# MLP of a hybrid decoder layer: order of a split, of copies and of one modulation changed

## The chip, the cores and the metric

The kernel runs on one core of one Trainium2 chip. The metric is the device time of one execution in microseconds. Three runs of the kernel before took 1068.99, 1073.79 and 1074.58 us (median 1073.79); the profiled execution took 1073.34 us.

## The reference

One decoder layer on 1024 tokens of 1024 channels, in float32:

```python
mod = (silu(c) @ ada_w + ada_b)
sh1, sc1, g1, sh2, sc2, g2 = split(mod, 6)
u = rmsnorm(h, norm_mix_w) * (1 + sc1) + sh1
...                                   # four token mixers on u @ w_in: pool, gated conv, SSD, S5
h = h + g1 * (groups @ w_out)
v = rmsnorm(h, norm_mlp_w) * (1 + sc2) + sh2
h = h + g2 * (square(relu(v @ w1)) @ w2)      # w1: 1024 x 4096, w2: 4096 x 1024
out = rmsnorm(h, final_norm_w)
```

The six vectors of the modulation are numbered s = 0 to 5 here: s = 3 is sh2, s = 4 sc2, and s = 5 is g2, the gate of the MLP.

## The kernel before

**Precision.** Every matrix operand is split into a high and a low part (ScalarE casts the high part, VectorE subtracts to get the low one: `split_w`, L114, and `split_half`, L1005 to L1007), and every product is three matmuls (`three`, L1078 to L1080): high by high, high by low, low by high.

**Order.** Nothing sets the order by hand but the program's text. A planner goes through the instructions by priority (their place in the text; those under `tc.high_priority()` come ahead of all others that are ready), simulates the engines, and fixes one order for each engine's queue and for SP's queue of DMA issues. On the chip each queue runs in that order. Buffers are slots of a tag with a fixed count (`BUFS`): "u" 16, "x" 8, "m" 4, "g5" 3 of 1024 columns, "s" and "t" 8 of 512; "w" 8 and "ws" 2 for weights. A tile waits for its slot until all readers of the earlier tile there are done. PSUM has eight banks, four of tag "pj" and four of "ms".

**Modulation.** Each of the six vectors is eight blocks of 128; a block is a load of 512 KB of `adaT` and one VectorE instruction with a running sum against `cond` (`ada_block`, L326). s = 0, 1, 2 and 4 are done early. The list `between` (L550) holds s = 5 and then s = 3; `ada_some(8)` takes the first eight after the S5 mixer, and `prepare` (L929) takes one more behind each of its w_out loads, through the same two "ws" buffers. `project` (L951) adds a group's output projection to h.

**v.** `to_v` normalises h for 128 tokens; after every fourth, `v_half` (L1012 on) transposes, and writes v's quarter operands "11", "21" (first half of the tokens), then "12", "22". The difference x12 - x11 and those after it, and their splits into operands T1 to T4, are made in `combinations` (L1028), called after the first weight pair.

**MLP, first product.** Sixteen pairs of weight blocks: pair 0 plainly, pairs 1 to 15 by a scheme of seven products in place of eight (`hidden`, L1099). A pair has three stages, divided by `yield`: the first multiplies "11" (bank `px`) and "21" (`py`); the second T2 (into `px` again) and T1 (`pz`), and T3 (into `px` again); the third T4 (into `px`) and "22" (into `pz`). Before a product is added into `px`, ScalarE copies what stands there (`u1`, L1125; `u2`, L1138; `u3`, L1147), and the next matmul into `px` waits for that copy. Each product is 12 matmuls of 512 columns. A pair's two raw weight tiles are "g5" tiles where n is even, "ws" tiles where it is odd (loads at L1105). A pair's results (squared ReLU and their sums) are stored to DRAM (L1058) for the second product. The loop at L1168 runs stage 2 of pair n, stage 1 of n + 1, stage 3 of n.

**MLP, second product.** Again seven products, in steps (`Step`, L1190) of 24 matmuls into four banks `q`. A step loads its operands a and b (L1182) into "u" tiles, splits them into four tiles of 1024 columns, "w" by default, and sets aside t12 = b12 - b11 in an "x" tile; loads run four steps ahead, splits two. T1 and T2 of the first product are in "x" tiles too, T3 in "m".

Of the kernel before, what the change touches and what calls it, by code (L numbers as in the profile page):

```python
# [16 lines left out]
ADD, SUB, MUL = ALU.add, ALU.subtract, ALU.mult  # L17
# [3 lines left out]
NB = 8  # L21
# [30 lines left out]
def body(ctx: ExitStack, tc: tile.TileContext, x, c, pk, adaT, w_x, w_zd, w_pl, w_gl, w_in, w_out, w1, w2, fnw, out):  # L52
    nc = tc.nc
    V, A, PE, G, SY = nc.vector, nc.scalar, nc.tensor, nc.gpsimd, nc.sync
# [8 lines left out]
    def gran(name, dt=F32, tag="m"):  # L63
        return gp.tile([P, 1024], dt, tag=tag, name=name, bufs=BUFS[tag])

    def half(name, dt=F32, tag="s"):
        return gp.tile([P, 512], dt, tag=tag, name=name, bufs=BUFS[tag])
# [4 lines left out]
    def small(name, w):  # L72
        return sm.tile([P, w], F32, tag=name, name=name)
# [4 lines left out]
    H = (slice(0, 512), slice(512, 1024))  # L78
# [56 lines left out]
    def tt(a, b, op, o=None, eng=None):  # L135
        if o is None:
            o = tmp(a.shape[1])
        (eng or V).tensor_tensor(out=o, in0=a, in1=b, op=op)  # L138
        return o
# [168 lines left out]
    cond = gran("cond")  # L308
# [6 lines left out]
    mod = small("mod", 48)  # L315
# [231 lines left out]
                PE.matmul(ps[h], w_[:, ks], u_[:, H[h]], start=(a and first), stop=(b and last))  # L547


    between = [(s_, j) for s_ in (5, 3) for j in range(NB)]  # L550

    def ada_some(n):
        for s_, j in between[:n]:
# [48 lines left out]
    for h in range(2):  # L602
        if h == 0:
            ps = [bank(f"pjx{i}{h}", "pj" if i < 4 else "ms") for i in range(NX)]
        for k in range(NB):
            if h == 0:
                t = load_xw(k)
# [27 lines left out]
            for i in range(NX):  # L635
                wh, wl, o = xw_of(k, i)
# [31 lines left out]
    for b in range(2):  # L668
        ps = proj(8 + b, f"s5{b}")
        v8_ = Vt[b].rearrange("p (m c) -> p c m", m=8)  # L670
        for h in range(2):
# [3 lines left out]
                     in_=Vt[b].rearrange("p (m c) -> p m c", m=8))  # L675
# [167 lines left out]
    def norm_of(grp, y, eps, tag):  # L843
        ps = bank(f"bss{grp}", "pj")
        sq = [gran(f"sq{grp}{b}", tag=tag) for b in range(2)]
        for h in range(2):
            for b in range(2):
                A.activation(out=sq[b][:, H[h]], in_=y[b][h], func=AF.Square)
            tt(sq[0][:, H[h]], sq[1][:, H[h]], ADD, o=sq[0][:, H[h]])
        for tb in range(NB):  # L850
            PE.matmul(ps[:, tb:tb + 1], sq[0][:, tb * P:(tb + 1) * P], one, start=True, stop=True)
        r = small(f"br{grp}", 8)
        V.tensor_scalar(out=r, in0=ps[:, 0:8], scalar1=1.0 / 256, scalar2=eps, op0=MUL, op1=ADD)
        G.tensor_tensor(out=r, in0=r, in1=mhalf.to_broadcast([P, 8]), op=ALU.pow)
        return r
# [73 lines left out]
    def prepare(grp, y, last=False):  # L929
        yh, yl = [], []  # L930
        for b in range(2):
            if last:
                hi, lo = ([half(f"y{n_}{grp}{b}{h}", F32R, t_) for h in range(2)] for n_, t_ in ("hs", "lt"))
            else:
                hi, lo = (gran(f"y{n_}{grp}{b}", F32R, "u") for n_ in "hl")
                hi, lo = ([t[:, H[h]] for h in range(2)] for t in (hi, lo))
            for h in range(2):
                A.copy(out=hi[h], in_=y[b][h])
                V.tensor_tensor(out=lo[h], in0=y[b][h], in1=f(hi[h]), op=SUB)
            yh.append(hi)  # L940
            yl.append(lo)
        wo = []
        for b in range(2):
            kb = grp * 2 + b
            t = load_w(w_out[kb], f"wo{kb}")
            V.scalar_tensor_tensor(out=t, in0=t, scalar=pv("bw", kb, kb + 1), in1=g1row, op0=MUL, op1=MUL)
            wo.append(split_w(t, f"wo{kb}"))
            ada_some(1)
        return grp, yh, yl, wo

    def project(prep, r, after_tb=None):  # L951
        grp, yh, yl, wo = prep
        for tb in range(NB):
            ts_ = slice((tb % 4) * P, (tb % 4 + 1) * P)
            for h in range(2):
                ps = bank(f"o{grp}{tb}{h}", "pj")
                for b in range(2):
                    yh_, yl_ = yh[b][tb // 4][:, ts_], yl[b][tb // 4][:, ts_]
                    PE.matmul(ps, yh_, wo[b][0][:, H[h]], start=(b == 0), stop=False)  # L959
                    PE.matmul(ps, yh_, wo[b][1][:, H[h]], start=False, stop=False)  # L960
                    PE.matmul(ps, yl_, wo[b][0][:, H[h]], start=False, stop=(b == 1))  # L961
                hh = ht[tb][:, H[h]]
                if r is None:
                    tt(hh, ps, ADD, o=hh)
                else:
                    V.scalar_tensor_tensor(out=hh, in0=ps, scalar=r[:, tb:tb + 1], in1=hh, op0=MUL, op1=ADD)
            if after_tb is not None:
                after_tb(tb)
# [9 lines left out]
    pb = prepare(1, yb)  # L978
    rb = []
    project(pa, ra, lambda tb: rb.append(norm_of(1, yb, EPS, "m")) if tb == 3 else None)  # L980
    pc = prepare(2, [[t[:, H[h]] for h in range(2)] for t in yc], True)
    project(pb, rb[0])

# [15 lines left out]
    def operand(e, j):  # L999
        if (e, j) not in vop:  # L1000
            vop[e, j] = gran(f"v{e}_{j}", F32R, RTAG[e])
        t = vop[e, j]
        return t[:, H[0]], t[:, H[1]]

    def split_half(hi, lo, t):  # L1005
        A.copy(out=hi, in_=t)  # L1006
        V.tensor_tensor(out=lo, in0=t, in1=f(hi), op=SUB)  # L1007
# [18 lines left out]
            V.tensor_tensor(out=lo, in0=t, in1=f(hi), op=SUB)  # L1026

    def combinations():  # L1028
        for j in range(KQ):
            x11, x12, x21, x22 = (vx[e, j] for e in ("11", "12", "21", "22"))  # L1030
            tt(x12, x11, SUB, o=x11)
            tt(x22, x12, SUB, o=x12)
            tt(x22, x11, SUB, o=x22)
            split_half(*operand("T2", j), x22)
            tt(x21, x22, SUB, o=x21)
        for j in range(KQ):
            split_half(*operand("T1", j), vx["11", j])
        for e, x_ in (("T3", "12"), ("T4", "21")):
            for j in range(KQ):
                split_half(*operand(e, j), vx[x_, j])  # L1040
# [58 lines left out]
    def hidden(n):  # L1099

        tag = "ws" if n % 2 else "g5"
        t0, t1 = (gran(f"w1_{n}{e}", tag=tag) if tag == "g5" else
                  wp.tile([P, 1024], F32, tag=tag, name=f"w1_{n}{e}", bufs=2) for e in range(2))
        for e, t in enumerate((t0, t1)):
            SY.dma_start(out=t, in_=w1[2 * n + e])  # L1105
        l11, l12, l21, l22 = t0[:, H[0]], t0[:, H[1]], t1[:, H[0]], t1[:, H[1]]

        def split(nm, t):
            o = wp.tile([P, 1024], F32R, tag="w", name=f"wo{nm}_{n}", bufs=8)
            o = o[:, H[0]], o[:, H[1]]  # L1110
            with tc.high_priority():
                split_half(*o, t)
            return o

        def product(o, e, ps, first):
            for j in range(KQ):
                three(ps, [cut(t, j * P) for t in o], operand(e, j), first and j == 0, j == KQ - 1, not first)

        sum_ = lambda a, b, op, o: tt(a, b, op, o=o)
        c = {}  # L1120
        x_, y_, z_ = bank(f"px{n}", "pj"), bank(f"py{n}"), None
        o11, o12 = split("11", l11), split("12", l12)
        product(o11, "11", x_, True)
        u1 = half(f"u1_{n}", tag="t")
        A.copy(out=u1, in_=x_)  # L1125
        product(o12, "21", y_, True)
        c["11"] = tt(u1, y_, ADD, o=u1)
        squared(u1)
        with tc.high_priority():
            tt(l21, l22, ADD, o=l21)  # L1130
            tt(l21, l11, SUB, o=l11)
        s2, s1 = split("S2", l11), split("S1", l21)
        with tc.high_priority():
            tt(l12, l11, SUB, o=l12)
        yield
        product(s2, "T2", x_, False)
        u2 = half(f"u2_{n}", tag="s")
        A.copy(out=u2, in_=x_)  # L1138
        z_ = bank(f"pz{n}")
        product(s1, "T1", z_, True)  # L1140
        o22 = split("22", l22)
        with tc.high_priority():
            tt(l22, l11, SUB, o=l22)
        s3 = split("S3", l22)
        product(s3, "T3", x_, False)
        u3 = half(f"u3_{n}", tag="s")
        A.copy(out=u3, in_=x_)  # L1147
        c["22"] = tt(u3, z_, ADD, o=u3)
        squared(u3)
        yield  # L1150
        s4 = split("S4", l12)
        product(o22, "T4", x_, False)
        c["21"] = half(f"c21_{n}", tag="t")
        squared(c["21"], x_)
        product(s4, "22", z_, False)
        c["12"] = tt(u2, z_, ADD, o=u2)
        squared(u2)
        keep_sums(n, c)
        yield
# [8 lines left out]
    for n in range(1, NP - 1):  # L1168
        next(pairs[n])
        next(pairs[n + 1])  # L1170
        next(pairs[n])
    g2r = row_of(5, "g2row")[0]
    next(pairs[NP - 1])

# [85 lines left out]
        return rstd_of(ss, 1.0 / D, EPS, f"rsf{tb}")  # L1260

    s0, s1 = banks("q0_", "pj"), banks("q1_", "ms")
    p1 = [Step("11", "B11", s0, i, True) for i in range(NI)]
    p2 = [Step("12", "B21", s1, i, True) for i in range(NI)]
    s2 = []
    p5 = [Step("S1", "T1", s2, i, True) for i in range(NI)]
# [196 lines left out]
```

## Time and profile before

| | |
|---|---|
| median of three runs | 1073.79 us |
| profiled execution | 1073.34 us |
| its span | 1071.2 us |
| TensorE (PE) busy | 1024.1 us, 4806 matmuls |
| VectorE (DVE) busy | 764.5 us |
| ScalarE (ACT) busy | 499.3 us |
| mean granted TensorE clock | 0.986 of full |

The span is from the first to the last instruction on the core. Busy shares are of the span. PEclk is the granted TensorE clock as a share of full speed. Times of single instructions are counted from the span's start. The mixers take the first 395 us or so, v is made until about 463 us, the MLP's first product runs to about 754 us, the second to the end.

### The profile page before, as it was taken

What the parts mean: (1) busy time and instruction counts of PE and PEld (TensorE: products, weight loads), DVE (VectorE), ACT (ScalarE), POOL (GpSimd) and SP (SyncE); (2) the same over time, 40 slices, a digit from 0 to 9 for tenths busy, and PEclk for the clock granted to TensorE, in tenths of its full rate; (3) what the DMA queues carried; (4) which work ended last, traced back from release to release, by engine and by line L of the source; (5) the groups of instructions that cost most, each with busy time, mean ns of one, the idle gap of its engine ahead of it and who ended that gap; (6) DMA issues with size and microseconds to landing.
All of it is one profiled execution on the core that took longest, in us unless ns stands there. A gap on an engine that the chain in (4) does not pass through costs nothing.

```text
span 1071.2 us, 13218 instructions
## 1 busy us (share of the span) xinstructions
PE 1024.1 (96%) x4806; PEld 836.5 (78%) x4806; DVE 764.5 (71%) x1339; ACT 499.3 (47%) x829; POOL 47.8 (4%) x83
## 2 busy tenths in 40 slices
PE   4989999999999999899999999998999999999997
PEld 3778987776888888688888887886788887777885
DVE  8999958777888878975655656555644766568683
ACT  5634623316634336754645555554443443433542
POOL 2300000000010102000000000000000000000041
PEclk9999999999889999899999999999999999999999
DMA  9873311134611215034444443477975466787112
GB/s 358 320 260 114 118 33 31 63 98 147 250 65 60 79 51 205 21 138 147 151 145 148 157 148 131 153 285 264 387 263 196 156 194 201 253 301 233 55 79 79
DMA packets 61027, 175.08 MB, mean 163 GB/s; under 512 B 6401, under 2 KB 11009, under 8 KB 60962
## 3 DMA queue, kind: packets, MB, share of 16 engines
q1 hardware_dynamic: 60322, 173.07, 46.5%
q8 instruction: 38, 0.62, 0.3%
q10 hardware_dynamic: 576, 1.05, 0.3%
q14 instruction: 27, 0.22, 0.1%
q0 software_dynamic: 64, 0.11, 0.0%
HBM read 135.17 MB, written 39.04 MB: 163 GB/s over the span
## 4 chain that ended last, share of the span: by engine, by line
PE 67%; DVE 15%; DMA 12%; ACT 3%; issue 3%; POOL 1%; SPq 0%; POOLq 0%; DVEq 0%; ACTq 0%
PE q L1079 5%; PE q L1080 5%; PE q L1078 5%; PE px L1078 5%; PE px L1080 5%; PE px L1079 5%; DMA b12T<-in_w_dram 3%; PE o L959 3%; PE o L960 3%; PE o L961 3%; DMA b21B<-in_w_dram 3%; PE pjpl L547 2%; PE pjs L547 2%; PE pz L1079 2%; PE pz L1080 2%
## 5 line engine op out<-in xcount | busy, mean ns | idle before, releaser
L1079 PE MATMUL q<-l_BT,h_AS 128*128 128x512 f32 x192 | 75.2, 392 | 2.6 <-DVE l_BT L1007 2.6
L1080 PE MATMUL q<-h_BT,l_AS 128*128 128x512 f32 x192 | 74.8, 389 | 0.0
L1006 ACT CAST h_AS<-aS 128x1024 fp32r<-128x1024 f32 x32 | 33.6, 1054 | 83.2 <-PE q L1079 66.8
L1007 DVE TENSOR_TENSOR woS<-w,woS 128x512 fp32r<-128x512 f32 x60 | 41.3, 689 | 36.0 <-ACT woS L1006 36.0
L1078 PE MATMUL q<-h_BT,h_AS 128*128 128x512 f32 x192 | 64.0, 389 | 0.0
L1007 DVE TENSOR_TENSOR wo<-w,wo 128x512 fp32r<-128x512 f32 x45 | 31.0, 690 | 44.9 <-ACT wo L1006 44.9
L1006 ACT CAST woS<-w 128x512 fp32r<-128x512 f32 x60 | 37.1, 623 | 44.2 <-PE px L1080 27.7
L1007 DVE TENSOR_TENSOR l_A<-a,h_A 128x1024 fp32r<-128x1024 f32 x24 | 29.3, 1222 | 38.3 <-ACT h_A L1006 36.0
L1007 DVE TENSOR_TENSOR l_AS<-aS,h_AS 128x1024 fp32r<-128x1024 f32 x32 | 39.0, 1221 | 23.8 <-ACT h_AS L1006 23.8
L1006 ACT CAST wo<-w 128x512 fp32r<-128x512 f32 x45 | 27.9, 623 | 54.8 <-PE px L1080 41.8
L959 PE MATMUL o<-wh_wo,yh 128*128 128x512 f32 x128 | 52.9, 413 | 0.1
L1006 ACT CAST h_A<-a 128x1024 fp32r<-128x1024 f32 x24 | 25.3, 1053 | 57.2 <-PE q L1079 45.5
L960 PE MATMUL o<-wl_wo,yh 128*128 128x512 f32 x128 | 50.8, 397 | 0.0
L1078 PE MATMUL px<-vT,woS 128*128 128x512 f32 x120 | 47.6, 397 | 2.9 <-ACT u L1125 2.9
L961 PE MATMUL o<-wh_wo,yl 128*128 128x512 f32 x128 | 50.4, 397 | 0.0
L1079 PE MATMUL q<-l_BB,h_A 128*128 128x512 f32 x128 | 50.1, 391 | 0.3 <-DVE l_BB L1007 0.3
L1080 PE MATMUL q<-h_BB,l_A 128*128 128x512 f32 x128 | 49.8, 389 | 0.0
L1080 PE MATMUL px<-vT,woS 128*128 128x512 f32 x120 | 47.3, 394 | 0.0
L1079 PE MATMUL px<-vT,woS 128*128 128x512 f32 x120 | 47.3, 394 | 0.0
L1079 PEld LDWEIGHTS q<-l_BT,h_AS 128*128 128x128 f32 x192 | 36.0, 188 | 11.9 <-DVE l_BT L1007 4.5
L1061 ACT ACTIVATE u<-u 128x512 f32<-128x512 f32 x45 | 28.5, 632 | 33.3 <-DVE u L138 32.1
L1078 PE MATMUL q<-h_BB,h_A 128*128 128x512 f32 x128 | 42.4, 390 | 1.1 <-ACT h_BB L1006 1.1
(496 smaller groups left out, 2958.1 us busy)
## 6 DMA issues: line engine op xcount, KB each, us to landing
ada<-in_ada_dram SPq DMA_DIRECT2D x32, 512.0 KB, 5.3
aS<-spS SPq DMA_DIRECT2D x32, 512.0 KB, 4.4
w<-in_w_dram SPq DMA_DIRECT2D x30, 512.0 KB, 3.8
spS<-s SPq DMA_DIRECT2D x48, 256.0 KB, 2.2
a<-sp SPq DMA_DIRECT2D x24, 512.0 KB, 6.2
ws_ada<-in_ada_dram SPq DMA_DIRECT2D x16, 512.0 KB, 3.6
b21B<-in_w_dram SPq DMA_DIRECT2D x16, 512.0 KB, 6.3
b22T<-in_w_dram SPq DMA_DIRECT2D x16, 512.0 KB, 3.4
```

The costliest lines, as they stand in the source:

```text
L547: PE.matmul(ps[h], w_[:, ks], u_[:, H[h]], start=(a and first), stop=(b and last))
L959: PE.matmul(ps, yh_, wo[b][0][:, H[h]], start=(b == 0), stop=False)
L960: PE.matmul(ps, yh_, wo[b][1][:, H[h]], start=False, stop=False)
L961: PE.matmul(ps, yl_, wo[b][0][:, H[h]], start=False, stop=(b == 1))
L1006: A.copy(out=hi, in_=t)
L1007: V.tensor_tensor(out=lo, in0=t, in1=f(hi), op=SUB)
L1061: A.activation(out=c, in_=c if src is None else src, func=AF.Relu)
L1078: PE.matmul(ps, wh, ub, start=first, stop=False, skip_group_check=more)
L1079: PE.matmul(ps, wh, lb, start=False, stop=False, skip_group_check=more)
L1080: PE.matmul(ps, wl, ub, start=False, stop=last, skip_group_check=more)
```

## The change

It does five things. `between` holds only s = 3, so the first eight blocks are now those of s = 3 and `prepare` does none. s = 5 is computed in the loop over pairs, for n = 2 to 9, one block in each turn as two half loads of 256 KB into "t" tiles, with `cond` copied to a "g5" tile before. `combinations` makes x12 - x11 and its split T1 first and under precedence. The three copies of `px` get precedence. The first step of the second product takes "x" tiles in place of "w" tiles.

```diff
-    between = [(s_, j) for s_ in (5, 3) for j in range(NB)]
+    between = [(3, j) for j in range(NB)]
...
     project(pa, ra, lambda tb: rb.append(norm_of(1, yb, EPS, "m")) if tb == 3 else None)
+
+    g2c = small("g2c", 8)
+    cond2 = gran("cond2", tag="g5")
+    A.copy(out=cond2, in_=cond)
     pc = prepare(2, [[t[:, H[h]] for h in range(2)] for t in yc], True)
...
     def combinations():
+        with tc.high_priority():
+            for j in range(KQ):
+                x11 = vx["11", j]
+                tt(vx["12", j], x11, SUB, o=x11)
+                split_half(*operand("T1", j), x11)
         for j in range(KQ):
             x11, x12, x21, x22 = (vx[e, j] for e in ("11", "12", "21", "22"))
-            tt(x12, x11, SUB, o=x11)
             tt(x22, x12, SUB, o=x12)
             tt(x22, x11, SUB, o=x22)
             split_half(*operand("T2", j), x22)
             tt(x21, x22, SUB, o=x21)
-        for j in range(KQ):
-            split_half(*operand("T1", j), vx["11", j])
...
-        A.copy(out=u1, in_=x_)
+        with tc.high_priority():
+            A.copy(out=u1, in_=x_)
...
-        A.copy(out=u2, in_=x_)
+        with tc.high_priority():
+            A.copy(out=u2, in_=x_)
...
-        A.copy(out=u3, in_=x_)
+        with tc.high_priority():
+            A.copy(out=u3, in_=x_)
...
         next(pairs[n])
         next(pairs[n + 1])
+        if 2 <= n < 2 + NB:
+            j = n - 2
+            for h in range(2):
+                t = half(f"ada5_{j}{h}", tag="t")
+                SY.dma_start(out=t, in_=adaT[40 + j][:, H[h]])
+                V.scalar_tensor_tensor(out=t, in0=t, scalar=0.5, in1=cond2[:, H[h]], op0=MUL, op1=MUL,
+                                       accum_out=(mod if h else g2c)[:, 40 * h + j:40 * h + j + 1])
         next(pairs[n])
+    tt(mod[:, 40:48], g2c, ADD, o=mod[:, 40:48])
...
-    p1 = [Step("11", "B11", s0, i, True) for i in range(NI)]
+    p1 = [Step("11", "B11", s0, i, True, tag="w" if i else "x") for i in range(NI)]
```

## Rows read from the trace of the kernel before

**Rows 1.** The page's first lines: span, and busy time of each engine.
```profile
span 1071.2 us, 13218 instructions
PE 1024.1 (96%) x4806; PEld 836.5 (78%) x4806; DVE 764.5 (71%) x1339; ACT 499.3 (47%) x829; POOL 47.8 (4%) x83
```

**Rows 2.** Windows: stretch, length, busy PE PEld DVE ACT POOL, PEclk, DMA share, GB/s.
```profile
431.00:446.00 15.00, 14.65 (x73) 11.68 (x71) 14.81 (x24) 9.14 (x14) 0.00 (x0) 1.00 0.00 1
449.90:455.00 5.10, 4.82 (x11) 3.37 (x12) 5.10 (x10) 5.10 (x11) 0.00 (x0) 0.51 0.00 0
287.70:301.30 13.60, 13.60 (x58) 12.40 (x58) 9.78 (x18) 5.29 (x11) 4.32 (x4) 0.50 0.54 214
500.00:650.00 150.00, 149.72 (x661) 123.64 (x660) 93.35 (x143) 83.37 (x144) 0.00 (x0) 1.00 0.43 151
726.60:733.60 7.00, 6.96 (x23) 5.52 (x24) 5.09 (x7) 1.73 (x3) 0.00 (x0) 0.76 0.90 324
705.00:754.00 49.00, 44.02 (x192) 35.21 (x191) 25.82 (x34) 24.49 (x39) 0.00 (x0) 0.97 0.87 313
```

**Rows 3.** Waits of TensorE over the span: total us, times, longest.
```profile
PE py L1080 <- DVE wo L1007: 1.5, 3, 1.0
...
PE q L1078 <- ACT h_BB L1006: 1.1, 1, 1.1
PE px L1078 <- ACT u L1147: 1.0, 2, 0.7
```

**Rows 4.** Timeline of TensorE: start, length, instruction, idle time before it.
```profile
449.91 0.80 PE L1078 MATMUL pz<-vT,woS 128*128 128x512 f32 x1 [3.86 <-ACT vT L1006]
450.50 0.63 PE L1078 MATMUL py<-v,wo 128*128 128x512 f32 x1
...
451.83 0.80 PE L1080 MATMUL py<-v,wo 128*128 128x512 f32 x1 [0.27 <-DVE wo L1007]
...
704.64 0.39 PE L1080 MATMUL px<-v,wo 128*128 128x512 f32 x1
...
726.64 0.50 PE L1078 MATMUL px<-vT,woS 128*128 128x512 f32 x1 [2.87 <-ACT u L1125]
```

**Rows 5.** Timeline of ScalarE, 725 to 735 us.
```profile
725.48 0.63 ACT L1062 ACTIVATE u<-u 128x512 f32<-128x512 f32 x1
726.02 0.57 ACT L1125 COPY u<-px 128x512 f32<-128x512 f32 x1
...
734.05 1.04 ACT L1006 CAST h_BB<-b11B 128x1024 fp32r<-128x1024 f32 x1 [3.68 <-PE px L1080]
```

**Rows 6.** Timeline of VectorE, 433 to 457 us.
```profile
433.28 0.69 DVE L138 TENSOR_TENSOR vx<-vx,vx 128x512 f32<-128x512 f32 x1
...
454.10 2.50 DVE L1007 TENSOR_TENSOR vT<-vx,vT 128x512 fp32r<-128x512 f32 x4
```

**Rows 7.** VectorE's modulation blocks and a 512-column instruction of that kind: ns min/median/max.
```profile
L326 DVE SCALAR_TENSOR_TENSOR ws_ada<-ws_ada,cond x16: 1209/1220/1226, 229.1 to 369.5; 128x1024 f32<-128x1024 f32 x16
...
L541 DVE SCALAR_TENSOR_TENSOR s5v<-ydt,s5v x4: 684/686/692, 254.9 to 257.2; 128x512 f32<-128x512 f32 x4
```

**Rows 8.** DMA issues of the page: count, KB each, median us to landing.
```profile
spS<-s SPq DMA_DIRECT2D x48, 256.0 KB, 2.2
...
ws_ada<-in_ada_dram SPq DMA_DIRECT2D x16, 512.0 KB, 3.6
```

**Rows 9.** Timeline of VectorE, then of TensorE, 283 to 298 us.
```profile
283.44 1.22 DVE L326 SCALAR_TENSOR_TENSOR ws_ada<-ws_ada,cond 128x1024 f32<-128x1024 f32 x1
...
286.32 1.94 PE L851 MATMUL bss<-one,sq 128*128 128x1 f32 x14 [0.76 <-DVE sq L138]
```

**Rows 10.** Groups of VectorE and ScalarE, 470 to 700 us: busy, mean | idle before, releaser.
```profile
L138 DVE TENSOR_TENSOR w<-w 128x512 f32<-128x512 f32 x25 | 17.2, 692 | 9.6 <-DMA w<-in_w_dram 9.1
...
L1006 ACT CAST wo<-w 128x512 fp32r<-128x512 f32 x36 | 22.4, 623 | 45.8 <-PE px L1080 35.9 <-PE pz L1080 9.7
...
L1125 ACT COPY u<-px 128x512 f32<-128x512 f32 x12 | 6.8, 570 | 0.0
```

## The prediction

> **What bounds the kernel now.** I read the busy shares first, then who waits for whom on TensorE, then the windows, then the order of instructions around each long wait. TensorE is busy 1024.1 of 1071.2 us [rows 1], so no edit gains anything that does not fill a TensorE gap or lift its clock; VectorE at 71% and ScalarE at 47% have room on average. The steady part of the MLP shows how little is left there: from 500 to 650 us TensorE is busy 149.72 of 150 us, 661 matmuls, 0.227 us apart [rows 2]. The gaps are elsewhere: one of 3.9 us before `pz` (the product with T1) and one of 2.9 us before `px` (it waits for ScalarE's copy, L1125) [rows 4], 1.1 us before the first matmul of the second product, 1.0 us for copies L1147 [rows 3]. Two of them cost twice. After the gap at 445.9 to 449.9 us the granted clock is 0.51 from 449.9 to 455.0, and after the one that ends at 726.6 it is 0.76 over 7.0 us [rows 2]: the first nearly all at the lower of the two levels (1.2 GHz, a share of 0.50), the second half of the time. A third stretch at 0.50, 287.7 to 301.3 us, lies in the mixer [rows 2]. It has no long gap before it, but short matmuls, one-column ones among them [rows 9].
>
> **The sum's frame.** The profiled execution took 1073.34 us: its span of 1071.2 and 2.1 around it. The median of the three runs is 1073.79, so the two can be set equal. Runs between 1068.99 and 1074.58 make 0.5% (5.4 us) about what a measurement can tell from no change.
>
> **Copies given precedence, and the first step's slots: the change of phase.** `px` of the last pair has its first product done at about 705.0 us [rows 4], but its copy L1125 runs at 726.02, right behind two activations of another accumulator [rows 5]; the next product into the same bank waits for it until 726.64 [rows 4]. The copy itself is 0.57 us and needs only the bank. With precedence it can go at 705 to 706, 20 us ahead of need. What goes is the wait, 2.87, and the slow stretch behind it, 0.24 of 7.0 us = 1.7: together 4.6. Next in line is the second product's first matmul, which waits 1.1 us for `h_BB`: that cast sits idle 3.68 us until `px` frees one of the eight "w" slots [rows 5]. The change gives this step "x" slots, which held T1 and T2; those are free after the products with T1 and T2, ahead of those with T3 that free the "w" slots now. With the step's operands there early, its matmuls fill holes; of 1.1 and the 1.0 of L1147 I count 1.4. What then is late is the loads: from 705 to 754 the queues already move 313 GB/s at a share of 0.87 [rows 2]. A step's three loads are 1.5 MB per 24 matmuls (5.4 us), 290 GB/s, so they fit with little to spare. The "x" slots also hold the differences `t12`; four of them must now wait for the first step, which delays buffers that later loads need. Between 2 (these loads come late and give most back) and 6.7 (all of it), I take 6.0.
>
> **First difference split early.** From 431 to 446 us VectorE is busy 14.81 of 15 us [rows 2]. The difference x12-x11 is already made at 433.28; what comes late is its split (T1), the four subtractions at 454.10 [rows 6]. TensorE has a T1 matmul next in its order and stands behind it until 449.91; of the `py` matmuls behind it two could have gone before, but the third waits for a low part from VectorE even so, until 451.83 [rows 4]. With precedence, four casts and four subtractions of 0.60 each (2.4 us) move ahead of v's second half. TensorE then can do the 12 T1 matmuls, 2.7 us, before the gap. The question is what of the rest comes 2.4 us later. If all of it, the gain is 2.7 - 2.4 = 0.3, and if the four casts (2.1 us of ScalarE) hold the transposes' evictions as well, -1.8. If `py` starts as now, at 450.5, the gain is 2.7 and the slow clock too, 5.1 us x (1 - 0.51) = 2.5, in all 5.2; the whole gap and the clock would be 6.4. The nearest row, VectorE's window, speaks for the low end; TensorE's order, which alone kept it from `py`, for the high one. I take 2.5, near the middle of 0.3 and 5.2, with -1.8 and 6.4 as the ends.
>
> **Gate's modulation out of the mixer.** The eight blocks that are done first are now those of s=3, in the same slots and at the same price. What leaves are the eight between the loads of w_out: 8 x 1.22 = 9.8 us of VectorE and eight loads of 3.6 us on SP's queue [rows 7, 8], where the next w_out load stands behind them for one of two "ws" buffers. TensorE pays for that work in one place that the profile shows: at 283.44 us a block stands ahead of the sums `sq`, and `bss` waits 0.76 us for these [rows 9]. I take that and one block's length that the VectorE-paced run of small matmuls behind it gains: 2.0. The ends are -2 (TensorE's order is made anew, and a wait as long as `bss` plus one block comes back) and 7.6 (0.8, and the stretch at half clock, 13.6 us x 0.50 = 6.8, goes too).
>
> **The same work in the MLP.** 16 half loads (256 KB; 2.2 us for one of that size [rows 8]) and 16 half blocks at about 0.69 us (the nearest row of 512 columns, [rows 7]) make 11.0 us of VectorE, over eight pairs. From 500 to 650 VectorE is idle 57 of 150 us [rows 2], and ScalarE's casts there wait for TensorE to free a slot [rows 10]: the splits run ahead of TensorE, and that hides these blocks. Not free are three things. The copy `cond2` (about 1.0 us of ScalarE, as a 1024-column cast in [rows 5]) keeps one of three "g5" buffers until pair 9, so even pairs load w1 with two buffers, as odd ones do now. The half loads wait on SP's queue for a "t" buffer, and w1's loads and the spills wait behind them. A half block whose load is late holds VectorE's queue, as the sums of w1 do now, 9.1 us in all [rows 10]. TensorE's only waits of this kind are 1.5 us in three [rows 3]. I take -0.5; the ends are 0 and -8 (one wait of 1.0, the longest of the three, in each of eight pairs).
>
> Sum: 6.0 + 2.5 + 2.0 - 0.5 = 10.0, so 1073.3 - 10.0 = **1063.3 us**.
>
> **Rivals.** (a) *The early split only moves the wait*, and the mixer's order stays TensorE's: of the sum 4.6 is left, less 0.5, so 1069.2. For it speaks the saturated VectorE [rows 2]; against it, that TensorE's order, not the data, first held `py`. (b) *The slow stretch in the mixer goes as well*: 1063.3 - 6.8 = 1056.5. Against it: the short matmuls stay, and it came with no gap over 1 us. (c) *Late w1 loads*, the end -8 in place of -0.5: 1070.8. For it, TensorE waited for such splits already; against it, odd pairs live with two buffers and 661 matmuls lost 0.3 us in 150. (d) *The slower side: copies hold ScalarE's queue.* A copy placed right behind its product waits at the head of the queue until TensorE is done, and the casts behind it wait as well. Now the copies never wait (0.0 before the twelve L1125), while one kind of cast waits 35.9 us for `px` [rows 10]. If in each of 15 pairs the copies before T2 and T3 cost TensorE 0.75 us each (between the mean, 0.5, and the longest, 1.0, of the waits for splits [rows 3]), 22.5 us are lost: 1085.8. It makes the kernel slower by more than 0.5% from 0.53 us each on. Against it: between a product and the next into its bank lie 12 matmuls of another bank, 2.7 us, against 0.6 for a copy, and splits run several products ahead.
> The Trainium skill ("PSUM — Partial Sum Buffer", Engine vs sequencer instructions) says that ScalarE's and VectorE's queues are strict first-in, first-out and matmuls run in program order; by that rule (d) is open wherever a copy is placed early, and the trace agrees with it where the copy at 726.02 runs straight behind activations that it does not need.
>
> **How the numbers follow.** Chances: forecast 0.52, (a) 0.20, (b) 0.08, (c) 0.10, (d) 0.10. The forecast's own range is 1058 to 1068. Case (b), and the better ends of the unknown terms, reach to 1055; (a) and (c) with a poorer phase change reach to 1075; (d) is left out. Faster by over 0.5% (under 1068.4): nearly all of the forecast, a third of (a), all of (b), 0.66. Within it: the rest of (a) and most of (c), 0.24. Slower: (d), 0.10.
>
> **What would show it.** Right: no wait of TensorE for L1125 and no dip of the clock behind it; `h_BB` cast some 5 to 10 us earlier against the last pair; the gap before `pz` down to 1 to 2 us, the clock there undisturbed; the pairs still 0.227 us a matmul. Wrong: a gap of 3 to 4 us at the same place before T2 or `py` (rival a); new waits of `px` for copies or of `py` for splits in the steady part (c, d); a busy share of DMA near 1 with waits for `h_BB` behind the phase change.

## The result, and the profile after

The changed kernel takes **1057.05 us** (median of four runs, 1055.91 to 1058.23) against 1074.18 for the kernel before beside it; the ratio is 0.985, 95% interval 0.982 to 0.988. It is faster by more than 0.5% and 6.3 us better than the forecast: inside the whole range (1055 to 1075), but 1 us below the forecast's own (1058 to 1068). The profiled execution took 1057.61 us, 15.7 less than that of before. The page's first lines:

```profile
span 1055.8 us, 13256 instructions
PE 1018.0 (96%) x4806; PEld 832.1 (79%) x4806; DVE 765.3 (72%) x1356; ACT 500.8 (47%) x830; POOL 49.1 (5%) x83
```

Both kernels run 4806 matmuls, so the start of the n-th matmul can be compared by stage. Each column is what a kernel gains (minus) or loses against the profile of before within that stage, in us; "T1", "copies", "slots" and "gate" are kernels with one part of the change alone (the experiments below):

```
stage, n of matmul                      changed    T1  copies  slots   gate
start, 0 to 1350                          -0.35  -1.50   0.86   0.09   0.28
mixer, 1350 to 2100                       -4.13   0.11  -0.20   0.87  -4.18
v and its first products, 2100 to 2300    -5.11  -5.57   0.21  -0.12   0.56
pairs, 2300 to 3300                       -1.88   0.50  -0.87  -0.06  -1.43
change of phase, 3300 to 3500             -4.12  -0.09  -4.20  -3.48  -0.07
second product, 3500 to 4806               0.24  -0.49  -0.94  -0.23  -0.71
all                                      -15.35  -7.04  -5.14  -2.93  -5.55
```

Each column rests on one profile. The stages without an edit show up to 1.5 us of scatter here (up to 2.9 in the start of later profiles, where a stretch at half clock near 70 us comes and goes); the others carry the difference. Where TensorE waits now, from the view of its waits over the span (total us, times, longest):

```profile
PE px L1084 <- ACT u L1156: 1.4, 2, 0.7
...
PE m L1085 <- DVE v L1030: 0.8, 1, 0.8
...
PE q L1084 <- ACT h_BB L1010: 0.6, 1, 0.6
PE py L1084 <- ACT wo L1010: 0.5, 1, 0.5
```

Of the waits of before [rows 3, 4], those of `pz` for the T1 split (3.86), of `px` for the copy at the phase change (2.87) and of `py` for low parts from VectorE (1.5) are gone. L1156 is the old L1147; TensorE waits for it in the last two pairs alone. The windows answer to [rows 2]: mixer, the end of v, what follows it, the pairs, the phase change (columns as there).

```profile
287.70:301.30 13.60, 13.60 (x57) 11.52 (x57) 9.89 (x20) 4.36 (x11) 5.37 (x4) 0.62 0.47 183
438.00:446.00 8.00, 6.67 (x27) 4.46 (x25) 8.00 (x15) 2.25 (x5) 0.00 (x0) 1.00 0.22 67
446.00:455.00 9.00, 9.00 (x41) 7.44 (x40) 9.00 (x16) 9.00 (x18) 0.00 (x0) 1.00 0.16 60
500.00:650.00 150.00, 150.00 (x663) 124.23 (x663) 101.33 (x172) 83.97 (x141) 0.00 (x0) 1.00 0.51 179
...
690.00:739.00 49.00, 46.56 (x209) 37.56 (x208) 30.05 (x39) 25.87 (x42) 0.00 (x0) 1.00 0.87 318
```

Behind v the clock stays full (1.00 from 446 to 455 us, where 449.9 to 455.0 had 0.51), so it does at the phase change (1.00 against 0.97), and TensorE is never idle between 500 and 650 us. VectorE does 8 us more there, and nothing waits for it. TensorE's timeline shows what fills the old gap:

```profile
438.23 0.39 PE L1084 MATMUL pz<-vT,woS 128*128 128x512 f32 x1
...
440.00 0.50 PE L1085 MATMUL m<-v,wh_w 128*128 128x512 f32 x1
...
442.40 0.39 PE L1086 MATMUL pz<-vT,woS 128*128 128x512 f32 x1
443.62 0.50 PE L1085 MATMUL m<-v,wh_w 128*128 128x512 f32 x1 [0.83 <-DVE v L1030]
...
445.52 0.49 PE L1084 MATMUL py<-v,wo 128*128 128x512 f32 x1 [0.47 <-ACT wo L1010]
445.85 0.40 PE L1085 MATMUL py<-v,wo 128*128 128x512 f32 x1
446.09 0.44 PE L1084 MATMUL m<-v,wh_w 128*128 128x512 f32 x1
...
454.57 0.39 PE L1086 MATMUL py<-v,wo 128*128 128x512 f32 x1
```

Twelve T1 products run between 438.2 and 442.8 us, where `pz` began at 449.91 [rows 4]. This kernel is 4.5 us ahead when v begins; `py` goes on at 445.52, half a microsecond before the 446.0 that its old place (450.50) would be. VectorE's own work did come later. The matmul that waits for v's last low part starts at 443.62 here; in the kernel before it is this one:

```profile
444.60 0.50 PE L1079 MATMUL m<-v,wh_w 128*128 128x512 f32 x1 [0.35 <-DVE v L1026]
```

With the lead of 4.5 us taken into account, that is 3.5 us later now. TensorE does not lose them, because its order is another one. The T1 products fill the time before that low part. Behind the first two `py` matmuls stand 24 of pair 0 (`m`, from 446.09), which before came after `py` and the first of T2 (from 457.97); the third `py`, which waited for VectorE before, comes at 454.57 without a wait. At the phase change, ScalarE and then TensorE (L1132 is the old L1125):

```profile
692.81 0.57 ACT L1132 COPY u<-px 128x512 f32<-128x512 f32 x1
...
711.29 1.03 ACT L1010 CAST h_BB<-b11B 128x1024 fp32r<-128x1024 f32 x1
...
713.69 0.57 ACT L1132 COPY u<-px 128x512 f32<-128x512 f32 x1
```

```profile
692.73 0.39 PE L1084 MATMUL px<-v,wo 128*128 128x512 f32 x1
...
696.13 0.39 PE L1084 MATMUL px<-vT,woS 128*128 128x512 f32 x1
...
712.37 0.73 PE L1084 MATMUL q<-h_BB,h_A 128*128 128x512 f32 x2 [0.57 <-ACT h_BB L1010]
713.63 0.50 PE L1085 MATMUL q<-l_BB,h_A 128*128 128x512 f32 x1 [0.52 <-DVE l_BB L1011]
...
716.03 0.39 PE L1084 MATMUL px<-vT,woS 128*128 128x512 f32 x1
...
722.30 0.50 PE L1084 MATMUL px<-vT,wo 128*128 128x512 f32 x1 [0.68 <-ACT u L1156]
```

The first copy, 692.81, is that of the pair before the last: it stands while the last pair's first product (`px<-v,wo`, its last matmul from 693.2 on) is still under way, and 3.3 us ahead of the `px` at 696.13 that needs its bank. The last pair's copy is the one at 713.69, twenty microseconds after its product and 2.3 ahead of the `px` at 716.03. That is not the 705 that I had forecast for it, but TensorE no longer stands still: twelve matmuls of the second product lie ahead of that `px`, and their first cast comes 4.7 us before it, where it came 7.4 behind it [rows 4, 5].

### The profile page after: what moved, and what is told of

It reads as the page before. It is cut to its first block, busy times and chain, and to the rows that moved or that the text cites. A ratio compares the mean times of both kernels' runs of the same rounds, so it can differ in the third digit from the quotient of the medians.

```text
span 1055.8 us, 13256 instructions
## 1 busy us (share of the span) xinstructions
PE 1018.0 (96%) x4806; PEld 832.1 (79%) x4806; DVE 765.3 (72%) x1356; ACT 500.8 (47%) x830; POOL 49.1 (5%) x83
## 4 chain that ended last, share of the span: by engine, by line
PE 73%; DVE 12%; DMA 9%; issue 3%; ACT 2%; POOL 0%; SPq 0%; POOLq 0%; DVEq 0%; ACTq 0%
PE q L1085 5%; PE px L1084 5%; PE px L1086 5%; PE px L1085 5%; PE q L1086 5%; PE q L1084 5%; DMA b12T<-in_w_dram 3%; PE o L959 3%; PE o L961 3%; PE o L960 3%; DMA b21B<-in_w_dram 3%; PE pz L1086 2%; PE pz L1085 2%; PE pz L1084 2%; DVE ada L326 2%
## 5 line engine op out<-in xcount | busy, mean ns | idle before, releaser
L138 DVE TENSOR_TENSOR u<-u,pz 128x512 f32<-128x512 f32 x30 | 20.6, 687 | 38.5 <-ACT u L1156 28.5
L966 DVE SCALAR_TENSOR_TENSOR h<-o,br,h 128x512 f32<-128x512 f32 x48 | 35.6, 746 | 12.3 <-PE o L961 12.1
```

## Experiments

Each ran beside the kernel before on the same chip. "At equal clock" below is a run's time less (1 - its mean granted clock) x its span. That takes out what a half-clock stretch can cost; the part of a stretch in which TensorE stands idle, and the stretch at the very end, where it is nearly done, are taken out as well though they cost little. e1 to e4, e5 to e8 and e9 to e12 ran on three chips; the changed kernel itself ran again only beside the last four.

**One part alone.** e1 has only the early first difference, e2 only the precedence of the copies, e3 only the slots, e4 only the gate's modulation; their edits are the four parts of the diff above.

> Only the early split of the first difference is done; the rest is the kernel before. Theory: the 5.1 us that the changed kernel gains between 428 and 460 us come from this part alone, because the T1 products and what stands behind them no longer wait for VectorE: the matmuls from 460 us on come 5 us earlier and stay there, no stretch at half clock near 450 us, and the total is 1073.8 - 5 = 1069. The gap of 2.9 us before px at the phase change stays, and so does the mixer. Rival 1: the T1 part only moves the wait, and the gain there needs the early copy of u1 (which frees a bank for the next products): gain under 2 us, 1072 to 1074. Rival 2: VectorE's queue, not the T1 order, sets that stretch, so the moved splits delay v's second half: no gain or a loss.

Measured: 1066.47 us, ratio 0.992 (0.989 to 0.995). The v stage gains 5.57 us, and neither rival holds; of what lies below the 1069 expected, 1.5 us stand in the start, where nothing was edited.

> Only the precedence of the three accumulator copies is done; the rest is the kernel before. Theory: the wait of 2.9 us at the phase change and the slow clock behind it (1.7 us) go, and the two waits for low parts in the steady pairs (1.9 us together) as well: 4 to 6 us less, 1068 to 1070. The first matmul of the second product still waits about 1 us or more for its h_BB cast. Rival 1 (early copies hold ScalarE's in-order queue): splits come late in some pairs, and the steady pairs lose 0.5 us or more each: 1075 or more. Rival 2 (the steady waits went through the new order of loads, not through the copies): steady pairs as before, 2.5 to 4.5 us less from the phase change alone.

Measured: 1067.69, ratio 0.994 (0.991 to 0.996). The phase change gains 4.20; of the two steady waits that at 667 us goes and that near 590 us stays (0.69). Rival 1, copies that hold ScalarE's queue, does not come about: in the pairs no wait for a split is longer than 0.7 us. Its condition did not arise either: in the order of ScalarE's instructions the L1125 copies of the middle pairs have not moved (they stand 3.3 us ahead of their `px` in both kernels), and a copy L1147 moved ahead of one cast (0.5 us). The last pair's copy L1125 goes at 722.48 instead of 726.02.

> Only the first step of the second product is put into the other slots; the rest is the kernel before. Theory: the wait of px for its copy stays the first that TensorE meets, but its order can now put matmuls of the first step of the second product there; at most the 1.1 us before that step go: 0.5 to 1.5 us less, 1072 to 1073.5. Rival 1: the step's matmuls fill the hole before px too, so that most of 4 us comes from the slots and little from the copies: 1069 to 1070. Rival 2: the differences that shared these slots come late instead: 0.5 to 2 us more.

Measured: 1070.39, ratio 0.996 (0.995 to 0.998). Rival 1 holds: 3.48 us at the phase change from the slots alone. TensorE's order now has the first step's matmuls where it stood still for `px`; what is left is a wait of 1.0 for that step's own low part, and 1.1 for the next step's cast.

> Only the gate's modulation is moved from the mixer into the MLP; the rest is the kernel before. Theory: the mixer's 4.3 us come from this part alone (3.3 of them between 272 and 292 us), and the 16 half blocks in the MLP cost TensorE nothing or up to 1 us: 1069 to 1071. Rival 1: the mixer's gain is there, but the steady pairs lose 2 to 4 us to late loads without the early copies: 1072 to 1073. Rival 2: the mixer's gain is undone at the wait before v, since VectorE, not TensorE, sets when v begins: matmuls from 460 us on as before, 1073 to 1074.

Measured: 1066.73, ratio 0.993 (0.990 to 0.995). The mixer's 4.18 us are this part's; the pairs gain 1.43 where I had expected a cost.

The gains of the four add up to 20.7 us by stages, the changed kernel has 15.4. The phase change was gained twice (7.8 us in the four, 4.1 here), and can be had once; most of the rest of the difference lies in the second product (2.4 us gained in the four, 0.2 lost here), where the profiles scatter.

**One part taken out of the changed kernel.** e5 leaves out the copies' precedence, e6 the slots; e7 keeps the early first difference but not its precedence:

```diff
     def combinations():
-        with tc.high_priority():
-            for j in range(KQ):
-                x11 = vx["11", j]
-                tt(vx["12", j], x11, SUB, o=x11)
-                split_half(*operand("T1", j), x11)
+        for j in range(KQ):
+            x11 = vx["11", j]
+            tt(vx["12", j], x11, SUB, o=x11)
+            split_half(*operand("T1", j), x11)
```

> The changed kernel without the precedence of the accumulator copies; its three other parts stay. Alone, the copies gained 4.2 us at the phase change and the slots 3.5 us there, while the changed kernel with both gained 4.1. Theory (the two do the same thing twice: each gives TensorE work for the one hole of 2.9 us before px): without the copies only 0.5 us are lost at the phase change, and nothing in the steady pairs, since the moved gate work alone had already shrunk their waits to 0.3 us: 1057 to 1058.5. Rival 1 (the copies carry the phase change, and the slots' own 3.5 us need the old order of the pairs): 4 us lost, 1061. Rival 2 (the copies also carry the 1.9 us of the steady pairs): 2 to 2.5 us lost, 1059 to 1060.

Measured: 1055.87, ratio 0.985 (0.981 to 0.989). The phase change loses 0.67 us and the pairs 0.46 against the profile of the changed kernel. The first is the theory's size; in the pairs it expected nothing, and rival 2 four times as much. The median does not show this loss: at equal clock e5's mean, 1050.7, is the highest of the four of its chip (e6 1047.8, e7 1048.0, e8 1049.7).

> The changed kernel with the first step of the second product in its old slots; the other parts stay. Theory (the slots repeat what the copies give): the phase change loses at most 0.5 us against the changed kernel, as with the copies alone (4.2 gained there against 4.1): 1057 to 1058. Rival (the slots take away the 1.1 us before the step's first cast, which the copies alone leave): 1 to 2 us lost, 1058 to 1059.5.

Measured: 1055.12, ratio 0.984 (0.980 to 0.987); the phase change stands at -0.08 us against the changed kernel. The theory holds. The waits mostly change their names, as the view of waits from 450 to 745 us shows, e5 first and then e6:

```profile
PE q L1084 <- ACT h_BB L1010: 1.1, 1, 1.1
PE q L1085 <- DVE l_BB L1011: 1.0, 1, 1.0
PE px L1084 <- ACT u L1153: 1.0, 2, 0.7
```

```profile
PE px L1084 <- ACT u L1156: 1.4, 2, 0.7
PE px L1084 <- ACT u L1146: 1.1, 1, 1.1
```

3.1 and 2.5 us, where the changed kernel has 2.5 (0.6, 0.5 and 1.4). The 0.6 us more in e5 are what its phase change loses.

> The changed kernel with the first difference and its split still written ahead of the second differences, but without precedence over the other work of v. Theory (VectorE is full from 431 to 446 us, so that the place in its queue decides): the split comes late again, the gap of 4 us and the slow clock behind it come back at least in half: 2 to 5 us lost, 1059 to 1062. Rival (it was TensorE's order alone that held py, and writing T1 ahead of T2 mends that): under 1 us lost, 1057 to 1058.

Measured: 1053.67, ratio 0.984 (0.979 to 0.988). The theory is wrong and the rival right: the v stage is as in the changed kernel (-0.01 us). VectorE's timeline in e7 shows T1's low parts among v's own work without any precedence, the last two from 436.53 on:

```profile
429.07 0.68 DVE L1011 TENSOR_TENSOR vT<-vx,vT 128x512 fp32r<-128x512 f32 x1
...
430.88 0.68 DVE L1011 TENSOR_TENSOR vT<-vx,vT 128x512 fp32r<-128x512 f32 x1
...
436.53 1.28 DVE L1011 TENSOR_TENSOR vT<-vx,vT 128x512 fp32r<-128x512 f32 x2
```

**The half blocks.** e8 leaves the gate's 16 half loads and half blocks out of the MLP (they are in the mixer no more either, so a result is missing):

```diff
             for h in range(2):
-                t = half(f"ada5_{j}{h}", tag="t")
-                SY.dma_start(out=t, in_=adaT[40 + j][:, H[h]])
-                V.scalar_tensor_tensor(...)
+                V.tensor_copy(...)        # one column of cond2 for each h
```

> The changed kernel with the 16 half loads and 16 half blocks of the gate's modulation left out of the MLP (and of the mixer too); two small copies a pair stand for their results. Theory: their price in the steady pairs is 0 to 0.5 us, since VectorE is idle a third of the time there, so the matmuls from 460 to 700 us on run as in the changed kernel: 1056.5 to 1057.5 where the mixer keeps its time. Rival 1: they cost 1 us or more in hidden waits, which would show as a shorter stretch of pairs 2 to 9. Rival 2: the steady waits of the kernel before come back (0.6 and 1.3 us), because the half loads were what delayed something else: 1058 to 1059. Of the mixer: if its 4.3 us are the work taken out, it runs as in the changed kernel to 0.5 us; if they hang on the order that TensorE's matmuls are given, which this edit changes a little between 330 and 400 us, up to 2 us are lost or won there.

Measured: 1057.38, ratio 0.985 (0.981 to 0.989). Rival 2 holds for one of its two waits (by the stages; the median would fit the theory): the pairs are 0.92 us slower without the half blocks, and a wait of `py` for VectorE is back. All six profiles without half blocks have it between 583 and 591 us, at the same matmul, the 2788th (0.5 to 1.0 us lost), none of the eight with them. Ahead of it a load of w1 comes late: VectorE's sums for it, e8 first, then the changed kernel, which stands 3.6 us ahead at that point:

```profile
575.06 0.69 DVE L138 TENSOR_TENSOR w<-w 128x512 f32<-128x512 f32 x1 [1.25 <-DMA w<-in_w_dram]
```

```profile
570.70 0.69 DVE L138 TENSOR_TENSOR w<-w 128x512 f32<-128x512 f32 x1 [0.45 <-DMA w<-in_w_dram]
```

The load landed 4.3 us after its issue in e8 and 3.5 in the changed kernel; 3.8 to 4.4 us in the six profiles, 3.4 to 3.5 in seven of the eight. In the eighth, e9, it took 3.8, and the wait is gone all the same, so the load alone does not make it. Why it is quicker, and what else takes the wait away, no run shows. The mixer, where the edit gave TensorE another order, stayed within 0.25 us.

**The mixer and the clock.** e9 puts eight loads of 512 KB back between those of w_out, without their blocks; e10 has neither the slots nor the precedence that e7 leaves out; e11 leaves the gate's modulation where it was; e12 is the changed kernel again.

```diff
-    between = [(3, j) for j in range(NB)]
+    between = [(s_, j) for s_ in (3, 5) for j in range(NB)]
...
+            if s_ == 3:
+                ada_block(s_, j, t)
+            else:
+                V.tensor_copy(out=mod[:, 40 + j:41 + j], in_=t[:, 0:1])
```

> The changed kernel with eight more 512 KB loads put back between the loads of w_out in the mixer, each read by one copy of a single column, so that the loads are there and the eight 1.22 us blocks are not (nothing uses what the copies write). Theory (the mixer gains because the blocks leave VectorE): the mixer runs as in the changed kernel, matmuls at 400 us within 1 us of it once the stretch at half clock near 288 us is set aside (it lasted 10.2 us in four and 3.4 us in two profiles of kernels with this part of the change, 13.7 us in four without it): 1055 to 1058. Rival 1 (the w_out loads behind them on the queue come late): 2 to 4 us of the mixer's gain are lost, 1059 to 1061. Rival 2 (it is only the order that TensorE's matmuls are given, which any edit here remakes): a change of up to 2 us of either sign, with waits at other places than in either kernel.

Measured: 1055.63, ratio 0.986 (0.981 to 0.990). The theory holds: the mixer gains 6.88 us against the kernel before, e12's profile 7.38, with a half-clock stretch of the same 3.4 us in both. All but 0.5 us of the gain stays with all the loads in place, so it is the blocks on VectorE, not the queue.

> The changed kernel without the two things that brought nothing beside the others: the first step's slots, and the precedence over other work of the early first difference (it stays written ahead). Theory: both are worth nothing here, so the time is that of the changed kernel run beside it, to 1 us at equal clock (1048 to 1049.5 us with the half-clock stretches taken out; 1053 to 1058 as measured). Rival: each covers for the other's hole, and 2 us or more come back at the phase change or before v's products: 1058 to 1060.

Measured: 1051.36, ratio 0.982 (0.978 to 0.986); by stages v and phase change are the changed kernel's to 0.1 us. It is 2.0 us below the changed kernel beside it (1053.36), at equal clock 0.6 (means 1046.8 and 1047.4): the same time, with two edits fewer.

> The changed kernel with the gate's modulation left in the mixer as before; the other parts stay. Theory: the mixer's 4.3 us are lost, with the stretch at half clock back to 13.7 us, and nothing else: in the steady pairs the early copies remove one of the two waits (1.3 us) and 0.6 to 0.9 us stay: 1061 to 1063 (1052 to 1053.5 with the half-clock stretches taken out). Rival (without the half blocks VectorE has more room in the MLP, which gives 1 to 2 us back there): 1059 to 1060.5.

Measured: 1061.03, ratio 0.990 (0.987 to 0.993). The theory holds: the mixer loses 4.58 us against the changed kernel's first profile (7.8 against e12's) and the pairs 0.51.

> The changed kernel once more, on the same chip as the three runs beside it. Theory: the clock's stretch near 288 us differs from execution to execution, so the time falls between 1053 and 1061 us in steps of about 3.4 us half lost (1.7 us and multiples), and all executions agree to 1.5 us once half of the slow stretches is taken out (near 1049). Rival: the scatter has another source and stays 3 us or more when the clock is taken out.

Measured: 1053.36 (1049.49 to 1057.85), ratio 0.983 (0.979 to 0.988). At equal clock its six runs lie between 1046.3 and 1048.3: of 8.4 us of scatter 2.0 are left, so the clock makes most of it. The theory had 1.5 us left and times from 1053 up; two of the six are near 1049.5. The four runs of the first session average 1049.4 at equal clock, 2.0 above e12's, so that much between sessions is not the clock.

The window 281 to 303 us shows it. First the kernel before, then e11, the changed kernel, its repeat e12, e9 and e10:

```profile
281.00:303.00 22.00, 21.24 (x96) 18.55 (x96) 18.18 (x36) 11.98 (x28) 4.32 (x4) 0.69 0.61 242
```

```profile
281.00:303.00 22.00, 20.86 (x94) 18.24 (x93) 18.23 (x36) 11.79 (x28) 4.32 (x4) 0.69 0.60 238
```

```profile
281.00:303.00 22.00, 22.00 (x108) 18.94 (x108) 17.91 (x36) 12.76 (x31) 5.37 (x4) 0.77 0.58 221
```

```profile
281.00:303.00 22.00, 22.00 (x123) 18.99 (x122) 20.24 (x38) 15.17 (x38) 4.64 (x4) 0.92 0.65 239
```

```profile
281.00:303.00 22.00, 22.00 (x125) 19.22 (x124) 20.77 (x41) 14.51 (x36) 5.83 (x4) 0.92 0.70 269
```

```profile
281.00:303.00 22.00, 22.00 (x133) 18.98 (x132) 21.60 (x39) 14.21 (x36) 5.34 (x4) 1.00 0.62 233
```

A clock of 0.69 in 22 us is 13.6 us at half (22 x 0.31 / 0.5); all five profiles with the old mixer have 0.69. With the new one it is 0.77 in four (10.1 us), 0.92 in four (3.5 us) and 1.00 in one, and TensorE runs 108 to 110, 123 to 127 and 133 matmuls in the window instead of 93 to 97. The changed kernel's two profiles, one program, have 0.77 and 0.92.

## Why the prediction came out, step by step

Three of the four terms had the right sign and, in the main, the right place; the sizes were off, by stages of the profiles: phase change 6.0 taken, 4.1 measured; first difference 2.5 and 5.1; mixer 2.0 and 4.1; MLP -0.5 and +1.9. 10.0 against 15.2. It is luck that the sum stayed within the whole range: one term was 1.9 us too large, the other three together 7.1 too small. The time is close to rival (b)'s 1056.5, but (b)'s reason, the clock in the mixer, makes only 1.7 us of this profile's difference.

**Phase change.** The wait of `px` and its slow clock went (4.6), though not by a copy at 705: with precedence it still goes 17 to 20 us after its product, only ahead of the two activations that stood before it. The trace of before had shown such a place: the copy of the pair before the last stands 3.3 us ahead of the `px` that needs it.

```profile
704.27 0.57 ACT L1125 COPY u<-px 128x512 f32<-128x512 f32 x1
...
707.59 0.39 PE L1078 MATMUL px<-vT,woS 128*128 128x512 f32 x1
```

What failed in the sum is the 1.4 on top: I added the slots' gain to the copies', though both give TensorE work for one hole. Alone they gain 3.5 and 4.2 (e3, e2), together 4.1; waits of 1.1 for `h_BB` and 1.0 for L1147 turned into 0.6, 0.5 and 1.4. The loads that I feared were no matter: 318 GB/s from 690 to 739 us, TensorE waiting for none.

**First difference.** The mis-sized term. Between 0.3 (all behind it comes 2.4 us late) and 5.2 (`py` as before, clock kept) I took the middle, leaning on a VectorE busy 14.81 of 15 us [rows 2]. The upper end came out, 5.1. What failed is the weight given to the low end, in which a delay on VectorE is one for TensorE: v's last low part did come 3.5 us later, but TensorE had the twelve T1 products for that time, two `py` in their old place, and then 24 matmuls of pair 0 that its old order had put later. The high end is right in its sum and not in its reason, since ten of the twelve `py` do not go as before. e7 shows that even the precedence was not needed once T1 was written ahead of T2. Rival (a) is refuted: the only gaps left there are 0.83 and 0.47 us.

**Mixer.** Without the clock the size is about right: 4.13 us less 1.7 (a half-clock stretch shorter by 13.6 - 10.1 us, at half) leaves 2.4 for 2.0 forecast; e11 against e12, 7.8 us less 5.1, leaves 2.7. In part that is luck. The wait of 0.76 for `sq` is gone and 1.1 us is gained by the 1400th matmul (292 us in the kernel before), where I had put all of it; the other 1.3 comes further on, with no more to see there than one wait of TensorE at 306.8 us that is gone too:

```profile
PE sds L825 <- ACT btk L809: 0.4, 1, 0.4
```

What failed in the sum is the clock, put into rival (b) with a chance of 0.08 as a thing that stays whole or goes whole. It went in part in eight of nine profiles, and whole in e10. My reason against it, that the short matmuls stay, did not hold: they stayed (32 of one column in the window in every profile), and the stretch shrank. Why, no run shows.

**MLP.** The sign was wrong. No half block held VectorE's queue and no second "g5" buffer was missed: TensorE is busy 150.00 of 150 us. Both steady waits for low parts (1.3 us) vanished. The matmuls from 2300 to 3300 differ between the changed kernel and the others nearly at two places alone. At the 2788th the kernel before loses 0.59 us, and no profile with half blocks loses anything. At the 3124th (667 us in the kernel before) that kernel loses 1.28; the nine profiles with early copies lose nothing there, and the half blocks without them (e4, e5) still 0.45. So the half blocks did not cost, they took a wait away, and the copies, for which I had counted nothing here, another. By what path is open in both. Rival (c), late loads of w1, did not come about.

**Rival (d)**, copies at the head of ScalarE's queue, cost nothing visible (e2). The Trainium skill ("PSUM — Partial Sum Buffer", Engine vs sequencer instructions) has that queue strictly first in, first out; the trace does not speak against it. The rival was not put to the test, though. A copy that stands 17 to 20 us behind its product waits for nothing, and the pairs of e2 are 0.87 us faster, not 22.5 slower. Why the planner does not place the L1125 copies of the middle pairs earlier, though they have precedence, was not tried.

Of the 17 us between the medians about half is clock: (1 - clock) x span averages 15.6 to 15.9 us in the kernel before in three sessions, 7.7 and 6.0 us in the changed one's two. The forecast had 4.2 of it, in the stretches behind the two gaps (1.7 and 2.5). At equal clock e12 gains 9.3 us (1056.7 to 1047.4, means).

## What to carry to other kernels

Two edits that fill the same hole are worth one of them: list which stretch of the in-order engine each one fills before adding, and take one out again when both are in. Where moved work pushes back other work of a busy engine, ask which instruction the bound engine's order stands at and what else it can run there, not only how busy the mover is; writing the operand that is needed first ahead of the others did here all that a precedence did. And count a stretch at half clock as a term of its own, with its range over executions, since here it was half of the gain.

## What the runs showed of the hardware that was not expected

- The same program, with the same order of instructions, had the stretch at half clock in the mixer for 10.1 us in one profile and 3.5 in another (granted clock 0.77 and 0.92 over 281 to 303 us). TensorE had no idle time in that window in either, but short matmuls.
- In six of the fourteen profiles a further stretch at half clock, 3.4 us, begins between 962 and 978 us, from 0.2 us before to 1.1 us after the end of a wait of 1.8 to 2.5 us for `l_BB`; in the others (waits of 1.5 to 2.5 us, e6 and e7 with 2.5 among them) the same wait has none behind it.
- One load of 512 KB, at the same place of the program, landed 3.5 us after its issue in the changed kernel and 4.3 us in e8, which issues fewer loads; 3.8 to 4.4 us in all six profiles without the half loads, 3.4 to 3.8 in the eight with them.
